# Strassen's seven products in 24 of 32 expanding feed-forward weight panels

## The chip, the cores and the metric

The kernel runs on one core of a Trainium2 chip. The metric is the device time of one execution in microseconds, the median of the runs. The kernel before took 2153.86 us (three runs, 2152.88 to 2155.65).

## The reference, cut to what matters

The program computes two transformer-like blocks on a stream of 512 tokens with 1024 features, all in float32. The first block has two layers (a convolution layer and a layer with forgetting attention), and each of them ends in a squared-ReLU feed forward:

```python
hn = rmsnorm(h, ffn_norm[i])
h = h + jnp.square(jax.nn.relu(hn @ ffn_w1[i])) @ ffn_w2[i]   # w1: 1024 x 4096, w2: 4096 x 1024
gate = jax.nn.sigmoid(rmsnorm(h, ple_norm[i]) @ ple_w_gate[i])
h = h + gate * (p[i] @ ple_w_proj[i])
```

The change lies in the product `hn @ ffn_w1[i]` of both layers. The second block (recurrence, block attention, memory attention, gated feed forward) is left as it was.

## The kernel before

The stream lies feature-major: eight tiles `h[f]` of 128 features x 512 tokens. Float32 products are made of three float32r products. Each operand is split into a high part, rounded to float32r, and a low part, the rest; `mm3` (line 356) issues weight-high x input-high, weight-high x input-low and weight-low x input-high into one accumulation in PSUM.

Weights come in panels of 128 x 2048 float32 (1 MB), in the order of the list `_KEYS`. A panel of `w1` holds 256 output features for all eight input tiles, so it takes 8 x 2 x 3 = 48 matmuls of 512 columns. `load` (299) issues a panel's DMA on the SP queue into one of two raw buffers. `part` (307) splits it a quarter at a time: ScalarE (ACT) copies the quarter into the high part, VectorE (DVE) subtracts to get the low part. High and low parts have two buffers each, so a panel is split while the one before it is multiplied, and `panel` (347) starts that for the next panel.

`ffn` (826) goes through four chunks of 1024 hidden features (c = 0 to 3) in each of the two layers. A chunk is four `w1` panels and then four `w2` panels. After each `w1` output tile DVE takes it out of PSUM (maximum with 0, times the norm's per-token factor `rbc`), ACT squares it, and ACT and DVE split the result for `w2`. Of `w2`, DVE adds each tile to the stream. `pairs` (379) runs the first panel of a group input tile by input tile for both output tiles at once (`couter`, 371), the others output tile by output tile.

The order of every engine's instructions is fixed when the program is built. `Flow` (124) keeps an estimated clock for each engine; side work (splitting, squaring, norms) is written as generators that name what their next step waits for, and each matmul issued lets those steps in that are due by the estimate. `quiet` (221) holds a step until an engine is about to be free, for at most `HOLD` us. On the chip each engine runs its list in order and waits by semaphores. Tiles of 128 x 512 come from one pool of `NSLOT` slots that are used in turn.

The products `p[i] @ ple_w_proj[i]` of both layers are made early, by `ple_proj` (700). Layer 0's eight tiles stay on chip, layer 1's go to DRAM (`prd`) and are read back after layer 1's feed forward.

Of the kernel before, what the change touches and what calls it, by code (L numbers as in the profile page):

```python
# [8 lines left out]
F32 = mybir.dt.float32  # L9
# [63 lines left out]
class Engine:  # L73
    """an engine whose instructions are issued in the order of the trace, with an estimate of when each one ends"""
# [152 lines left out]
def kernel(ctx: ExitStack, tc, gain0, x_t, p_t, mem_t, vec, w, w_f, w_lru, rows, consts, out):  # L227
# [69 lines left out]
    raws, parts = {}, {}  # L297

    def load(i, pieces=1):
        if i < len(_KEYS) and i not in raws:  # L300
            r = wp.tile([128, PW], F32, name=nm("raw"), tag="raw", bufs=2)
            raws[i] = r
            c = PW // pieces
            return [lambda k=k: dma(r[:, c * k:c * k + c], w[i, :, c * k:c * k + c]) for k in range(pieces)]
        return []

    def part(i, k, pieces, low):
        """piece k of a panel's split, its low part on engine low"""
        if k == 0:
            parts[i] = tuple(wp.tile([128, PW], F32R, name=nm(n), tag=n, bufs=2) for n in ("hi", "lo"))  # L310
        r, (hi, lo), c = raws[i], parts[i], PW // pieces
        s = slice(c * k, c * k + c)
        gain = GAINED.get(_KEYS[i][0])
        if gain is not None:
            g = col(gain, k)
            act.activation(hi[:, s], r[:, s], AF.Copy, scale=g)
            dve.scalar_tensor_tensor(lo[:, s], r[:, s], g, hi[:, s].bitcast(F32), op0=ALU.mult, op1=ALU.subtract)
        else:
            act.copy(hi[:, s], r[:, s])
            low.tensor_sub(lo[:, s], r[:, s], hi[:, s].bitcast(F32))  # L320

    def splitting(i):
        pieces = KT if _KEYS[i][0] in GAINED else 4
# [17 lines left out]
    def prefetch(i, delay):  # L341
        for g in load(i) + load(i + 1):
            g()
        if i < len(_KEYS) and _KEYS[i] not in FULL32:
            ahead[i] = flow.spawn(splitting(i), delay, 2)
# [1420 lines left out]
```

## Time and profile before

| | |
|---|---|
| median of three runs | 2153.86 us |
| profiled execution | span 2154.4 us, the only time shown for it |
| TensorE (PE) busy | 2109.2 us, 98% of the span, 9920 matmuls |
| VectorE (DVE) busy | 1270.6 us, 59% |
| ScalarE (ACT) busy | 937.4 us, 44% |
| GpSimd (POOL) busy | 370.5 us, 17% |
| granted TensorE clock, mean | 0.993 of full |
| DMA | 204.79 MB, queue q1 busy 26.8% |

A matmul's listed duration is its way through the array, and matmuls overlap: what a row of them costs is read from the distance between their starts, not from the sum of the durations. The same holds, by less, on DVE and ACT, where a merged row of four like instructions is shorter than four times one.

### The profile page before, as it was taken

The numbers are of one execution on the slowest core, as the hardware profiler recorded it, in microseconds if no ns is written. First come the engines' busy times: TensorE is split into PE (matmuls) and PEld (weight loads), VectorE is DVE, ScalarE is ACT, GpSimd is POOL, SyncE is SP. The second block draws the span as 40 slices with busy tenths as digits, with TensorE's granted clock in tenths as the row PEclk, the third lists the DMA queues.
The fourth block names the chain that finished last, engine by engine and source line by source line (L and its number), as shares of the span: only waits on it lengthen the run. The fifth ranks groups of instructions, "written<-read, shape, count | busy, mean of one in ns | idle before, by whom it ended". The sixth has DMA issues, their size and how long they took to land. (4 is left out here: it accounts for less than half of the span.)

```text
span 2154.4 us, 26102 instructions
## 1 busy us (share of the span) xinstructions
PE 2109.2 (98%) x9920; PEld 1741.6 (81%) x9920; DVE 1270.6 (59%) x2166; ACT 937.4 (44%) x1884; POOL 370.5 (17%) x380
## 2 busy tenths in 40 slices
PE   7999999999999999999999999999999999999998
PEld 6867888888878887788888887778888888888887
DVE  5997534344576887544343567775564556465563
ACT  5766423233446676433232453665452333232222
POOL 5881100000121336300000031331010010000002
PEclk9999999999999999999999999999999999999999
DMA  5215232232222111222222233112222422222221
GB/s 183 98 45 190 86 110 80 97 104 92 98 80 85 61 61 60 79 98 98 98 93 89 95 125 129 71 64 95 98 79 79 142 93 98 100 96 98 95 101 59
DMA packets 38444, 204.79 MB, mean 95 GB/s; under 512 B 4648, under 2 KB 7976, under 8 KB 15920
## 3 DMA queue, kind: packets, MB, share of 16 engines
q1 hardware_dynamic: 37744, 202.62, 26.8%
q8 instruction: 78, 1.28, 0.2%
q10 hardware_dynamic: 576, 0.52, 0.1%
q14 instruction: 46, 0.38, 0.1%
HBM read 195.45 MB, written 7.68 MB: 94 GB/s over the span
## 5 line engine op out<-in xcount | busy, mean ns | idle before, releaser
L83 PE MATMUL mm<-xh,hi 128*128 128x512 f32 (+1 forms) x2544 | 991.5, 390 | 9.3 <-ACT hi L83 8.4
L83 PE MATMUL mm<-xl,hi 128*128 128x512 f32 (+1 forms) x2544 | 990.5, 389 | 0.0
L83 PE MATMUL mm<-xh,lo 128*128 128x512 f32 (+1 forms) x2544 | 990.0, 389 | 0.2
L83 PEld LDWEIGHTS mm<-xh,hi 128*128 128x128 f32 x2544 | 480.2, 189 | 105.0 <-ACT hi L83 8.4
L83 PEld LDWEIGHTS mm<-xh,lo 128*128 128x128 f32 x2544 | 480.1, 189 | 96.5 <-DVE lo L83 1.5
L83 PEld LDWEIGHTS mm<-xl,hi 128*128 128x128 f32 x2544 | 480.2, 189 | 94.3
L83 ACT CAST hi<-raw 128x512 fp32r<-128x512 f32 x636 | 354.3, 616 | 288.6 <-PE mm L83 268.9
L83 DVE TENSOR_TENSOR lo<-raw,hi 128x512 fp32r<-128x512 f32 x584 | 387.9, 713 | 50.3 <-ACT hi L83 48.8
L83 POOL TENSOR_TENSOR sq<-sq,sq 128x512 f32<-128x512 f32 (+1 forms) x69 | 84.7, 1230 | 1330.0 <-ACT sq L83 1329.4
L83 DVE TENSOR_TENSOR h<-mm,h 128x512 f32<-128x512 f32 (+1 forms) x113 | 75.6, 671 | 279.7 <-PE mm L83 279.6
L83 ACT ACTIVATE z<-z 128x512 f32<-128x512 f32 x64 | 40.4, 631 | 205.3 <-DVE z L83 205.3
L83 DVE SCALAR_TENSOR_TENSOR z<-mm,rbc 128x512 f32<-128x512 f32 x64 | 44.0, 690 | 120.7 <-PE mm L83 120.7
L83 POOL TENSOR_SCALAR P<-P,s 128x128 f32<-128x128 f32 (+2 forms) x112 | 65.3, 588 | 243.6 <-DVE s L83 151.0
L83 DVE TENSOR_TENSOR t<-mm,rbc 128x512 f32<-128x512 f32 x80 | 54.9, 688 | 82.5 <-PE mm L83 78.7
L83 DVE TENSOR_TENSOR xl<-z,xh 128x512 fp32r<-128x512 f32 x64 | 44.3, 693 | 74.7 <-ACT xh L83 74.7
L83 ACT ACTIVATE t<-t 128x512 f32<-128x512 f32 x40 | 25.2, 631 | 128.5 <-DVE t L83 128.4
L83 POOL TENSOR_TENSOR acc<-acc,tap 128x482 f32<-128x482 f32 (+29 forms) x60 | 77.3, 1288 | 13.1 <-ACT tap L83 9.5
L83 DVE SCALAR_TENSOR_TENSOR sc<-u,V,sc 128x511 f32<-128x511 f32 (+21 forms) x116 | 78.9, 732 | 0.5
L83 ACT ACTIVATE xh<-h,V 128x512 fp32r<-128x512 f32 x40 | 28.6, 722 | 112.4 <-DVE h L83 112.4
L83 POOL TENSOR_TENSOR lo<-raw,hi 128x512 fp32r<-128x512 f32 x52 | 69.6, 1363 | 38.8 <-ACT hi L83 38.6
L83 ACT CAST pth<-ptp 128x128 fp32r<-128x128 f32 (+2 forms) x112 | 46.1, 418 | 53.2 <-PE ptp L83 52.6
L83 ACT ACTIVATE P<-sc,s 128x128 f32<-128x128 f32 (+2 forms) x112 | 58.5, 524 | 18.1 <-DVE s L83 17.4
(228 smaller groups left out, 2235.8 us busy)
## 6 DMA issues: line engine op xcount, KB each, us to landing
raw<-in_w SPq DMA_DIRECT2D x175, 1024.0 KB
h<-in_x_t SPq DMA_DIRECT2D x8, 256.0 KB
prd<-pr SPq DMA_DIRECT2D x8, 256.0 KB
pr<-prd SPq DMA_DIRECT2D x8, 256.0 KB
resid<-h SPq DMA_DIRECT2D x8, 256.0 KB
h<-resid SPq DMA_DIRECT2D x8, 256.0 KB
out<-out SPq DMA_DIRECT2D x12, 128.0 KB
raw<-in_w SPq DMA_DIRECT2D x4, 256.0 KB
```

The costliest lines, as they stand in the source:

```text
L83: f(out, *args, **kw)
```

## The change

Strassen's scheme multiplies 2 x 2 blocks with seven block products instead of eight, and pays with sums of blocks. Here the blocks are: of the inputs, the even and odd feature tiles times the two halves of 256 tokens; of a weight panel, its two output tiles times the even and odd input tiles. It is used for the `w1` panels of chunks 1 to 3 in both layers (`SEVEN`, 24 of 32). Chunk 0 keeps the old products, since the input sums are made meanwhile.

A panel's columns are now stored as four blocks of 512 columns (`blocks`, on the host, a permutation only). For a panel of `SEVEN`:

- `sums_split` makes four sums of blocks on DVE and splits them: four high parts on ACT, four low parts on DVE. Three blocks (a11, a12, a22) are also used alone; ACT makes their high parts.
- `lows_by_dma` makes those three blocks' low parts without DVE: ACT writes minus the rounded block into the low tile, and a DMA issued from POOL adds the block, read again from DRAM, to that tile (`accum_op=ALU.add`).
- `seven` issues seven products of four input tiles each, 3 matmuls of 256 columns per tile: 84 matmuls into three PSUM banks, of which two are added up in place. Between products ACT copies three half tiles out of PSUM, and DVE subtracts in PSUM twice, subtracts once on the way out, and applies the factor `rbc` to four half tiles.
- `combos` makes, once per layer during chunk 0, the sums of the inputs: for each of four pairs of tiles two scaled copies (ACT), four half-width sums (DVE), and the splits of two tiles.

High and low parts get one tile for each block (still two buffers). `NSLOT` grows from 60 to 64. Layer 0's `ple_proj` tiles go to DRAM as well, and both layers' are read back before the last chunk's `w2` panels (`pr_load`). Comments are dropped.

```diff
+    raws, parts, early = {}, {}, {}
 
     def load(i, pieces=1):
         if i < len(_KEYS) and i not in raws:
+            if _KEYS[i] in SEVEN:
+                early[i] = flow.spawn(lows_by_dma(i), 0.0, 2)
...
+    spent = set()
+    cur = [0]
+    def accumulate(out, src):
+        nc.gpsimd.dma_start(out, src, accum_op=ALU.add)
+        flow.dma_t = max(flow.dma_t, flow.now, flow.when([out])) + 4 * out.size() / 175e3
+        for k in flow.spans(out):
+            flow.ready[k] = flow.dma_t + 2.5
+    def lows_by_dma(i):
+        r = raws[i]
+        for b in range(3):
+            c = slice(S * b, S * b + S)
+            yield lambda: cur[0] >= i - 1 or (i - 2, b) in spent
+            yield r[:, c]
+            yield flow.quiet(act, patience=HOLD)
+            if i not in parts:
+                parts[i] = Panel(_KEYS[i])
+            lo = parts[i].piece("lo", b)
+            act.mul(lo, r[:, c], -1.0)
+            yield lo
+            accumulate(lo, w[i, :, c])
+    def sums_split(i):
+        if i not in parts:
+            parts[i] = Panel(_KEYS[i])
+        pan, r = parts[i], raws[i]
+        a11, a12, a22, a21 = (r[:, S * b:S * b + S] for b in range(4))
+        yield r
+        f1, f2, f3, f4 = (slot(p="sum") for _ in range(4))
+        pan.sums = tuple(mid(3 * S, F32R, n) for n in ("sh", "sl"))
+        def both(b):
+            return [t[:, S * b:S * b + S] for t in pan.sums]
+        s1, s2, s3, s4 = [pan.piece("hi", 3), pan.piece("lo", 3)], both(0), both(1), both(2)
+        pan.s1, pan.s2, pan.s3, pan.s4 = s1, s2, s3, s4
+        wait = lambda e: flow.quiet(e, patience=HOLD_SUMS)
+        yield wait(dve)
+        dve.tensor_add(f1, a21, a22)
+        yield wait(act)
+        act.copy(pan.piece("hi", 0), a11)
+        yield wait(dve)
+        dve.tensor_add(f2, f1, a11)
+        for f, (hi, lo), nxt, raw in (
+                (f2, s2, lambda: dve.tensor_add(f3, a11, a21), None),
+                (f1, s1, lambda: dve.tensor_add(f4, f2, a12), 1),
+                (f3, s3, None, 2), (f4, s4, None, None)):
+            yield f
+            yield wait(act)
+            act.copy(hi, f)
+            if nxt:
+                yield wait(dve)
+                nxt()
+            yield hi
+            yield wait(dve)
+            dve.tensor_sub(lo, f, hi.bitcast(F32))
+            if raw:
+                yield wait(act)
+                act.copy(pan.piece("hi", raw), r[:, S * raw:S * raw + S])
...
+    def combos(xs, src, g, out):
+        for j in range(KT // 2):
+            a, b = 2 * j, 2 * j + 1
+            yield lambda: xs[a] is not None and xs[b] is not None
+            yield [src[a], src[b], *xs[a], *xs[b]]
+            ga, gb = slot(p="ga"), slot(p="gb")
+            for t, f in ((ga, a), (gb, b)):
+                yield flow.quiet(act, patience=HOLD)
+                act.activation(t, src[f], AF.Copy, scale=g(f))
+            yield [ga, gb]
+            u, t = slot(p="u13"), slot(p="tu")
+            lh, rh = slice(0, HALF), slice(HALF, S)
+            for o, p, q, op in ((u[:, lh], ga[:, lh], ga[:, rh], dve.tensor_sub),
+                                (u[:, rh], ga[:, rh], gb[:, rh], dve.tensor_sub),
+                                (t[:, lh], gb[:, rh], u[:, lh], dve.tensor_add),
+                                (t[:, rh], gb[:, lh], t[:, lh], dve.tensor_sub)):
+                yield flow.quiet(dve, patience=HOLD)
+                op(o, p, q)
+            two = []
+            for z in (u, t):
+                zh, zl = slot(F32R, "ch"), slot(F32R, "cl")
+                yield z
+                yield flow.quiet(act, patience=HOLD)
+                act.copy(zh, z)
+                yield zh
+                yield flow.quiet(dve, patience=HOLD)
+                dve.tensor_sub(zl, z, zh.bitcast(F32))
+                two.append((zh, zl))
...
+    def seven(key, xs, cx, post):
+        pan = panel(key)
+        i = _PIDX[key]
+        lh, rh = slice(0, HALF), slice(HALF, S)
+        n = len(cx)
+        x = lambda f, h: [tuple(t[:, h] for t in xs[2 * j + f]) for j in range(n)]
+        y = lambda f, h: [tuple(t[:, h] for t in cx[j][f]) for j in range(n)]
+        block = lambda b: (pan.piece("hi", b), pan.piece("lo", b))
+        def product(ps, wt, bs, start):
+            for j in range(n):
+                c = slice(128 * j, 128 * j + 128)
+                a, b = (t[:, c] for t in wt)
+                p, q = bs[j]
+                pe.matmul(ps, a, p, start=start and j == 0, stop=False, skip_group_check=True)
+                pe.matmul(ps, a, q, start=False, stop=False, skip_group_check=True)
+                pe.matmul(ps, b, p, start=False, stop=j == n - 1, skip_group_check=True)
+        r1, r6 = bank()[:, :HALF], bank()[:, :HALF]
+        c1, c5 = slot(p="p1"), slot(p="n5")
+        c1, cw, c5 = c1[:, lh], c1[:, rh], c5[:, lh]
+        product(r1, block(0), x(0, lh), True)
+        spent.add((i, 0))
+        act.copy(c1, r1)
+        product(r6, pan.s2, y(1, lh), True)
+        full = bank("sc", 2)
+        r5 = full[:, :HALF]
+        dve.tensor_sub(r6, r6, c1)
+        act.copy(cw, r6)
+        product(r5, pan.s1, y(0, lh), True)
+        act.copy(c5, r5)
+        dve.tensor_sub(r5, r5, cw)
+        product(r1, block(1), x(1, lh), False)
+        spent.add((i, 1))
+        post(0, lh, r1)
+        product(r6, pan.s3, y(0, rh), False)
+        post(1, rh, r6, c5)
+        product(r5, pan.s4, x(1, rh), False)
+        post(0, rh, r5)
+        release("sc", full)
+        product(r6, block(2), y(1, rh), False)
+        post(1, lh, r6)
...
+            ahead[i] = flow.spawn(splitting(i), 0.2 if _KEYS[i] in SEVEN else delay, 2)
 
     def panel(key, fetch=True):
         i = _PIDX[key]
+        cur[0] = max(cur[0], i)
         if i not in ahead:
             ahead[i] = flow.spawn(splitting(i), 0.0, 2)
         flow.finish(ahead[i])
+        if i in early:
+            flow.finish(early[i])
...
+        cx = [None] * (KT // 2)
+        pr = None
         for c in range(4):
             z = [None] * KT
-            for k, ps in pairs([("w1", l, c, i) for i in range(4)], front.xs):
+            keys = [("w1", l, c, i) for i in range(4)]
+            for k, ps in pairs([q for q in keys if q not in SEVEN], front.xs):
                 rbc = front.get()
                 t = slot(p="z")
                 dve.scalar_tensor_tensor(t, ps, 0.0, rbc, op0=ALU.max, op1=ALU.mult)
                 flow.spawn(squared(z, k, t), 0.0, 0)
+                if c == 0 and k == 1:
+                    made = flow.spawn(combos(front.xs, h, front.g, cx), 0.0, 2)
+            if c == 0:
+                flow.finish(made)
+            for i, key in enumerate(keys):
+                if key not in SEVEN:
+                    continue
+                two = [slot(p="z") for _ in range(2)]
+                done = []
+                def post(j, half, ps, sub=None):
+                    t = two[j][:, half]
+                    if sub is not None:
+                        dve.tensor_sub(t, ps, sub)
+                        ps = t
+                    dve.scalar_tensor_tensor(t, ps, 0.0, front.rbc[:, half], op0=ALU.max, op1=ALU.mult)
+                    done.append(j)
+                    if done.count(j) == 2:
+                        flow.spawn(squared(z, 2 * i + j, two[j]), 0.0, 0)
+                seven(key, front.xs, cx, post)
+            if c == 3:
+                pr = pr_load(l)
...
+    def pr_load(l):
+        pr = []
+        for f in range(KT):
+            t = slot(p="pr")
+            dma(t, prd[KT * l + f])
+            pr.append(t)
+        return pr
...
-NSLOT = 60
+NSLOT = 64
...
+HOLD_SUMS = 0.6
+BLOCKED = ("w1",)
+SEVEN = {("w1", l, c, i) for l in range(2) for c in range(1, 4) for i in range(4)}
...
+    def blocks(m):
+        m = m.reshape(128, 4, 2, 2, 128)
+        return np.concatenate([m[:, :, o, t].reshape(128, 512) for o, t in ((0, 0), (1, 0), (1, 1), (0, 1))], axis=1)
...
-            return wide(a["ffn_w1"][key[1]], 1024 * key[2] + 256 * key[3], 256)
+            return blocks(wide(a["ffn_w1"][key[1]], 1024 * key[2] + 256 * key[3], 256))
```

In the orders below, `xh`, `xl` are the parts of the input tiles, `ch`, `cl` those of the input sums, `hi`, `lo` the parts of weight blocks, `sum` a weight sum before it is split, and `sh`, `sl` the parts of three of the four weight sums.

TensorE, the second `w1` panel of layer 0's chunk 1 in the kernel before, its first two input tiles:

```order
L83 MATMUL mm433_2662<-xh319_1775,hi428_2613 128x512
L83 MATMUL mm433_2662<-xl320_1776,hi428_2613 128x512
L83 MATMUL mm433_2662<-xh319_1775,lo429_2614 128x512
L83 MATMUL mm433_2662<-xh321_1777,hi428_2613 128x512
L83 MATMUL mm433_2662<-xl322_1778,hi428_2613 128x512
L83 MATMUL mm433_2662<-xh321_1777,lo429_2614 128x512
```

and the first panel of that chunk now: the end of the first product and the start of the second.

```order
L83 MATMUL mm598_2829<-xh417_1988,lo580_2740 128x256
L83 MATMUL mm598_2829<-xh434_2072,hi591_2760 128x256
L83 MATMUL mm598_2829<-xl435_2073,hi591_2760 128x256
L83 MATMUL mm598_2829<-xh434_2072,lo580_2740 128x256
L83 MATMUL mm599_2830<-ch470_2241,sh587_2753 128x256
L83 MATMUL mm599_2830<-cl471_2242,sh587_2753 128x256
L83 MATMUL mm599_2830<-ch470_2241,sl588_2754 128x256
L83 MATMUL mm599_2830<-ch493_2325,sh587_2753 128x256
L83 MATMUL mm599_2830<-cl494_2326,sh587_2753 128x256
L83 MATMUL mm599_2830<-ch493_2325,sl588_2754 128x256
```

Matmuls of 512 columns have become ones of 256, three for each pair of blocks as before; the second product takes sums on both sides, and its three parts take turns as those of the first do.

VectorE, from one output tile of the first `w1` panel of that chunk to the split of the second next panel, before:

```order
L83 SCALAR_TENSOR_TENSOR z430_2656<-mm426_2596,rbc365_2066 128x512
L83 SCALAR_TENSOR_TENSOR z431_2658<-mm427_2597,rbc365_2066 128x512
L83 TENSOR_TENSOR xl435_2667<-z430_2656,xh434_2666 128x512
L83 TENSOR_TENSOR xl437_2674<-z431_2658,xh436_2673 128x512
L83 TENSOR_TENSOR lo439_2689<-raw425_2594,hi438_2688 128x512 x4
L83 SCALAR_TENSOR_TENSOR z440_2707<-mm433_2662,rbc365_2066 128x512
L83 TENSOR_TENSOR xl443_2719<-z440_2707,xh442_2718 128x512
L83 SCALAR_TENSOR_TENSOR z444_2739<-mm441_2709,rbc365_2066 128x512
L83 TENSOR_TENSOR xl448_2751<-z444_2739,xh447_2750 128x512
L83 TENSOR_TENSOR lo450_2765<-raw432_2660,hi449_2764 128x512 x4
```

and now, the second panel's products and the third panel's sums and splits:

```order
L83 TENSOR_TENSOR mm625_2977<-mm625_2977,p1626_2978 128x256
L83 TENSOR_TENSOR xl638_3002<-z596_2826,xh637_3001 128x512
L83 TENSOR_TENSOR sl634_2990<-sum630_2986,sh633_2989 128x512
L83 TENSOR_TENSOR sc640_3028<-sc640_3028,p1626_2978 128x256
L83 TENSOR_TENSOR sum632_2988<-sum630_2986,raw597_2827 128x512
L83 TENSOR_TENSOR lo636_2992<-sum629_2985,hi635_2991 128x512
L83 SCALAR_TENSOR_TENSOR z621_2972<-mm624_2976,rbc453_2162 128x256
L83 TENSOR_TENSOR sl634_2990<-sum631_2987,sh633_2989 128x512
L83 TENSOR_TENSOR z622_2973<-mm625_2977,n5627_2979 128x256
L83 SCALAR_TENSOR_TENSOR z622_2973<-z622_2973,rbc453_2162 128x256
L83 TENSOR_TENSOR sl634_2990<-sum632_2988,sh633_2989 128x512
L83 SCALAR_TENSOR_TENSOR z621_2972<-sc640_3028,rbc453_2162 128x256
```

Between two panels stood two 512-wide outputs (`z`), two low parts of outputs (`xl`) and the four quarters of one panel. Now the half-wide steps on `mm` and `sc` stand between the sums and the low parts of the next panel, and each waits for its product while those behind it wait in the queue.

ScalarE in the same place, before:

```order
L83 ACTIVATE z430_2656<-z430_2656 128x512
L83 CAST xh434_2666<-z430_2656 128x512
L83 ACTIVATE z431_2658<-z431_2658 128x512
L83 CAST xh436_2673<-z431_2658 128x512
L83 CAST hi438_2688<-raw425_2594 128x512 x4
L83 ACTIVATE z440_2707<-z440_2707 128x512
L83 CAST xh442_2718<-z440_2707 128x512
L83 ACTIVATE z444_2739<-z444_2739 128x512
L83 CAST xh447_2750<-z444_2739 128x512
L83 CAST hi449_2764<-raw432_2660 128x512 x4
```

and now, in the first panel of the chunk:

```order
L83 COPY p1600_2831<-mm598_2829 128x256
L83 CAST sh609_2848<-sum606_2845 128x512
L83 COPY p1600_2831<-mm599_2830 128x256
L83 CAST hi611_2850<-sum605_2844 128x512
L83 COPY n5601_2832<-sc614_2881 128x256
L83 CAST hi615_2907<-raw578_2736 128x512
L83 CAST sh609_2848<-sum607_2846 128x512
L83 ACTIVATE lo616_2916<-raw597_2827 128x512
L83 CAST hi617_2925<-raw578_2736 128x512
L83 ACTIVATE lo618_2933<-raw597_2827 128x512
L83 CAST sh609_2848<-sum608_2847 128x512
L83 ACTIVATE z595_2825<-z595_2825 128x512
```

The three copies `p`, `p`, `n` from PSUM have come in, and the negative copies `lo<-raw` of the third panel (`raw597`) stand in the queue while the first panel is multiplied. The added DMAs follow each other on POOL, whose list in this place held nothing for the feed forward:

```order
L83 TENSOR_TENSOR s445_2135<-s444_2134,mhalf_78 128x4
L361 DMA lo580_2740<-in_w 128x512
L361 DMA lo581_2743<-in_w 128x512
L361 DMA lo582_2746<-in_w 128x512
L361 DMA lo602_2834<-in_w 128x512
L361 DMA lo603_2837<-in_w 128x512
L361 DMA lo604_2840<-in_w 128x512
```

The first row is the norm's factor; behind it stand three transfers for each panel.

## Rows read from the trace of the kernel before

**Rows 1.** the page: span, busy time by engine, granted TensorE clock in 40 slices

```profile
span 2154.4 us, 26102 instructions
PE 2109.2 (98%) x9920; PEld 1741.6 (81%) x9920; DVE 1270.6 (59%) x2166; ACT 937.4 (44%) x1884; POOL 370.5 (17%) x380
...
PEclk9999999999999999999999999999999999999999
```

**Rows 2.** waits, 250 to 600 us: waiter <- releaser, us, times, longest

```profile
DVE h L83 <- PE mm L83: 92.5, 25, 5.1
DVE z L83 <- PE mm L83: 58.9, 24, 7.1
...
PEld tp L83 <- POOL s L83: 0.4, 1, 0.4
```

**Rows 3.** timeline of TensorE, layer 0's feed forward: start, duration; 21 rows

```profile
379.32 0.39 PE L83 MATMUL mm<-xl,hi 128*128 128x512 f32 x1
...
383.85 0.39 PE L83 MATMUL mm<-xh,hi 128*128 128x512 f32 x1
```

**Rows 4.** timeline of TensorE in a stretch of 256-column matmuls; 59 rows

```profile
664.92 0.28 PE L83 MATMUL mm<-lo,xh 128*128 128x256 f32 x1
...
671.88 0.28 PE L83 MATMUL mm<-hi,xl 128*128 128x256 f32 x1
```

**Rows 5.** timeline of VectorE in two w1 panels: start, busy, idle before

```profile
359.57 0.69 DVE L83 SCALAR_TENSOR_TENSOR z<-mm,rbc 128x512 f32<-128x512 f32 x1 [2.71 <-PE mm L83]
...
370.45 0.69 DVE L83 SCALAR_TENSOR_TENSOR z<-mm,rbc 128x512 f32<-128x512 f32 x1 [2.71 <-PE mm L83]
372.49 0.69 DVE L83 TENSOR_TENSOR xl<-z,xh 128x512 fp32r<-128x512 f32 x1 [1.35 <-ACT xh L83]
373.10 2.49 DVE L83 TENSOR_TENSOR lo<-raw,hi 128x512 fp32r<-128x512 f32 x4
```

**Rows 6.** groups of VectorE: busy us, mean ns of one, idle before

```profile
L83 DVE TENSOR_TENSOR lo<-raw,hi 128x512 fp32r<-128x512 f32 x584 | 387.9, 713 | 50.3 <-ACT hi L83 48.8 <-DMA h<-resid 1.2
...
L83 DVE TENSOR_TENSOR xl<-z,xh 128x512 fp32r<-128x512 f32 x64 | 44.3, 693 | 74.7 <-ACT xh L83 74.7
...
L83 DVE TENSOR_TENSOR h<-xh,xl 128x512 f32<-128x512 f32 x4 | 6.2, 1607 | 0.0
...
L83 DVE SCALAR_TENSOR_TENSOR out<-h,V,tp 128x256 f32<-128x256 f32 x12 | 4.9, 476 | 3.2 <-ACT rbc L83 3.2
...
L83 DVE TENSOR_TENSOR h<-mm,h 128x256 f32<-128x256 f32 x8 | 3.4, 422 | 12.4 <-PE mm L83 12.4
```

**Rows 7.** timeline of ScalarE in the same panel as the last of rows 5

```profile
372.37 2.18 ACT L83 CAST hi<-raw 128x512 fp32r<-128x512 f32 x4
```

**Rows 8.** groups of ScalarE, columns as in rows 6

```profile
L83 ACT CAST hi<-raw 128x512 fp32r<-128x512 f32 x636 | 354.3, 616 | 288.6 <-PE mm L83 268.9 <-issue 18.6 <-DMA raw<-in_w 0.9
...
L83 ACT ACTIVATE z<-z 128x512 f32<-128x512 f32 x64 | 40.4, 631 | 205.3 <-DVE z L83 205.3
L83 ACT CAST xh<-z 128x512 fp32r<-128x512 f32 x64 | 39.8, 621 | 2.3
...
L83 ACT ACTIVATE xh<-h,V 128x512 fp32r<-128x512 f32 x40 | 28.6, 722 | 112.4 <-DVE h L83 112.4
...
L83 ACT CAST pth<-ptp 128x256 fp32r<-128x256 f32 x40 | 14.7, 372 | 25.0 <-PE ptp L83 24.9
```

**Rows 9.** busy time by stretch: PE, PEld, DVE, ACT, POOL, clock, DMA share, GB/s

```profile
250.00:600.00 350.00, 350.00 (x1553) 289.81 (x1552) 152.07 (x234) 119.31 (x210) 9.21 (x7) 1.00 0.28 96
353.00:364.00 11.00, 11.00 (x50) 9.10 (x49) 5.30 (x9) 4.59 (x8) 0.00 (x0) 1.00 0.26 97
...
344.00:348.00 4.00, 4.00 (x19) 3.34 (x18) 0.76 (x2) 1.25 (x2) 0.00 (x0) 1.00 0.74 262
```

**Rows 10.** the page's DMA issues: queue, count, KB each

```profile
raw<-in_w SPq DMA_DIRECT2D x175, 1024.0 KB
```

**Rows 11.** groups of GpSimd, columns as in rows 6

```profile
L83 POOL TENSOR_TENSOR s<-s,mhalf 128x4 f32<-128x4 f32 x10 | 12.8, 1284 | 53.6 <-DVE s L83 53.6
```

More of the change, by code (lines that the diff above doesn't have):

```diff
@@ L305, in load, with __init__, piece, cols @@
         return []
-    def part(i, k, pieces, low):
[L309 to L312, printed above, removed]
+    class Panel:
+        def __init__(self, key):
+            self.key, self.blocked = key, key[0] in BLOCKED
+            self.q = {}
+        def piece(self, n, b):
+            if (n, b) not in self.q:
+                self.q[n, b] = wp.tile([128, S], F32R, name=nm(n), tag=f"{n}{b}", bufs=2)
+            return self.q[n, b]
+        def cols(self, a, m):
+            return tuple(self.piece(n, a // S)[:, a % S:a % S + m] for n in ("hi", "lo"))
+        def weights(self, k, c0, width, m):
+            if self.blocked:
+                return self.cols(S * (c0 // 128 * (3 - k % 2) + (1 - c0 // 128) * (k % 2)) + k // 2 * 128, m)
+            return self.cols(k * width + c0, m)
+    class Plain:
+        def __init__(self, hi, lo):
+            self.hi, self.lo = hi, lo
+        def weights(self, k, c0, width, m):
+            a = k * width + c0
+            return self.hi[:, a:a + m], self.lo[:, a:a + m]
+    def part(i, k, pieces, low):
+        if i not in parts:
+            parts[i] = Panel(_KEYS[i])
+        c = PW // pieces
+        r = raws[i][:, c * k:c * k + c]
+        hi, lo = parts[i].cols(c * k, c)
         gain = GAINED.get(_KEYS[i][0])
@@ new lines, in sums_split @@
+    def sums_split(i):
+        if i not in parts:
+            parts[i] = Panel(_KEYS[i])
+        pan, r = parts[i], raws[i]
[30 more added lines that the diff above has]
+                act.copy(pan.piece("hi", raw), r[:, S * raw:S * raw + S])
@@ new lines, in combos @@
+    def combos(xs, src, g, out):
[26 more added lines that the diff above has]
+                two.append((zh, zl))
+            out[j] = two
@@ L322, in splitting @@
     def splitting(i):
+        if _KEYS[i] in SEVEN:
+            yield from sums_split(i)
+            return
         pieces = KT if _KEYS[i][0] in GAINED else 4
@@ L367, in gemm @@
                 flow.until(lambda: xs[k] is not None)
-            a = k * width + c0
-            mm3(ps, hi[:, a:a + m], lo[:, a:a + m], xs[k][0], xs[k][1], k == 0, k == n - 1)
+            wh, wl = pan.weights(k, c0, width, m)
+            mm3(ps, wh, wl, xs[k][0], xs[k][1], k == 0, k == n - 1)
     def couter(pan, xs, ks=None, banks=None):
@@ L688 @@
             conv_pe(k)
-    prd = dp.tile([KT, 128, S], F32, name="prd")
+    prd = dp.tile([2 * KT, 128, S], F32, name="prd")
     def gemm32(ps, raw, c0, xs, width, m=128):
@@ L715, in ple_proj @@
             act.copy(t, ps)
-            res.append(t)
-            if not keep:
-                dma(prd[f], t)
-            elif f in PLE_PE:
+            dma(prd[KT * l + f], t)
+            if l == 0 and f in PLE_PE:
                 conv_pe(PLE_PE[f])
-        return res
     memd = dp.tile([4, 128, S], F32, name="memd")
@@ L1271 @@
     front = Front(lambda f: gg[:, f:f + 1])
-    pr = []
-    for f in range(KT):
-        t = slot(p="pr")
-        dma(t, prd[f])
-        pr.append(t)
     def to_second(f):
```

34 lines of the change are left out of this document (16 added, 18 removed).

## The prediction

> **What bounds the kernel now.** First the page's head: TensorE is busy for 98% of the span, VectorE for 59%, ScalarE for 44%, and the clock slices stand at 9 throughout [rows 1]. Matmuls overlap, so a busy TensorE need not be a full one; the busy table of the first feed forward says more: from 250 to 600 us PE has work in all of the 350 us at a granted clock of 1.00 (the 2.4 GHz level), while DVE works 152 and ACT 119 us [rows 9]. Then the waits of that stretch: DVE waits for PE's sums (92.5 and 58.9 us in its two largest rows), and the only wait of the PE side is 0.4 us, in a norm [rows 2]. So in the feed forward nothing but the pace of the matmuls sets the time, and what the change takes off that pace comes off the span, as long as DVE, ACT and the transfers keep up.
>
> The pace itself is read from the timeline by starts. 512-column matmuls start every (383.85 - 379.32) / 20 = 0.2265 us [rows 3], and the same tile of two successive `w1` panels leaves at 359.57 and 370.45: 10.88 us per panel, 0.2267 for each of its 48 matmuls [rows 5]. 256-column matmuls of the same kind start every (671.88 - 664.92) / 58 = 0.120 us [rows 4], though every one of them has other weights than the one before it (high, low, high of the next tile). That is more than half of 0.2267: about 0.0133 us of each matmul does not shrink with its columns.
>
> **What the change removes on TensorE.** A panel of `SEVEN` had 48 matmuls of 512 columns, 10.88 us. It now has 7 products x 4 tiles x 3 = 84 of 256 columns: 84 x 0.120 = 10.08 us. The saving is 0.80 us, not the eighth (1.36 us) that the columns alone would give. 24 panels: 19.2 us. Nothing else on PE changes in number.
>
> **What it adds on VectorE, for each panel.** Before: 4 low parts, 2 outputs, 2 splits, 5.30 us of work in an 11 us window [rows 9]. Now 4 sums, 4 low parts of sums, 2 splits of outputs (10 full-width operations), 3 half-width subtractions and 4 half-width outputs. Price from below: four low parts in a row take 2.49 us, the last of them as long as a single one, 0.69, so each holds the engine (2.49 - 0.69) / 3 = 0.60 us [rows 5]; the half-width rows last 0.422 (two operands) and 0.476 us (three) [rows 6], less the same tail of 0.09 us 0.33 and 0.39. That is 10 x 0.60 + 3 x 0.33 + 4 x 0.39 = 8.6 us. From above, whole durations without overlap: 8 x 0.713 + 2 x 0.693 + 3 x 0.422 + 4 x 0.476 = 10.3 us. The panel's new pace on PE is 10.08, so DVE has either 1.5 us to spare or none. I take 8.6 (within a panel DVE's queue is mostly full, and back to back is then the right price), plus something for waits: the half-width steps wait for their products with sums queued behind them, as DVE's order shows.
>
> **On ScalarE, for each panel.** 3 negative copies, 3 plain high parts, 4 high parts of sums, 2 squares, 2 high parts of outputs (14 full-width), and 3 half-width copies from PSUM. From below: (2.18 - 0.62) / 3 = 0.52 us each [rows 7], and 0.372 - 0.095 = 0.28 for the half ones [rows 8]: 8.1 us. From above: 10 x 0.616 + 2 x 0.631 + 2 x 0.621 + 3 x 0.372 = 9.8 us. It fits below 10.08 in both cases; before it was 4.59 in 11 us [rows 9].
>
> **Hand-overs between products.** The tightest is bank r6: after the fifth product DVE must take r6 minus c5 out before the seventh adds to it. One product lies between, 12 x 0.120 = 1.44 us; the subtraction takes 0.42, so about 1.0 us is left for what stands ahead of it on DVE. One full-width operation (0.69) fits, a second costs PE some 0.4 us. For 24 panels this is between 0 and 10 us. I take 1.2 us (0.05 each): the order puts one low part and one half-width output between the neighbouring hand-overs, not two low parts. The other hand-overs have two products (2.9 us) or more.
>
> **The added transfers.** 3 per panel, 256 KB each, read and added to what is in SBUF, issued from POOL. The trace has no transfer that adds and none from POOL. From below: a plain 1 MB panel [rows 10] takes 0.74 x 4 us = 2.96 us of all 16 engines [rows 9], so 256 KB take 0.74 us. From above: four passes instead of one, 2.96 us, and in series with it an issue as long as the longest small POOL row, 1.28 us [rows 11], together 4.2 us. The middle that I take is two passes, 1.5 us.
>
> The Trainium skill, "Collectives: The Full Stack", section "The bandwidth ceiling: the fold count and why AG ≠ RS ≠ AR", says that an adding transfer is slower because it reads two sources, not because of the adding. By that page a transfer here would be an estimated 1.5 us; no row here shows it.
>
> At 1.5 us a panel needs 3 x 1.5 + 2.96 for the next raw panel = 7.5 of 10.08 us of the DMA engines; this fits. Latency doesn't matter: ACT's order shows the third panel's negative copies queued between the first panel's own copies, so a low part is started more than one panel (10 us) ahead of its product. On POOL nothing for the feed forward is queued behind these transfers; its busy time in the stretch is 9.21 us of 350 [rows 9].
>
> **Edits at nothing.** `combos`, once per layer: ACT 8 x 0.722 + 8 x 0.62 [rows 8] = 10.7 us, DVE 16 x 0.42 + 8 x 0.69 [rows 6] = 12.3 us, in a chunk 0 of 8 x 10.88 = 87 us where both engines are idle more than half of the time [rows 9]; should they wait, the first panel of chunk 1 is late by a part of that. Sixteen reloads and eight more stores of 256 KB, 6 us of transfers per layer, stand on SP ahead of a raw panel that is loaded a panel (10.88 us) early; DMA share there is 0.28 [rows 9]. At each chunk's end the last panel finishes both its output tiles together, but the first `w2` panel uses them last, 6 x 6 x 0.2267 = 8.2 us after it starts.
>
> **The sum.** 2154.4 (the profiled span; it stands 0.5 us above the median of the runs) - 19.2 + 1.2 = 2136.4, so about **2136 us**, 0.8% faster. Of this the pace of the matmuls is sure, the 1.2 us is judgement.
>
> **Rivals.**
>
> *VectorE sets the panel's pace.* For it: 8.6 us of work in 10.08 us, in strict order, behind hand-overs with ACT and PE at every second step; the low parts' mean of 0.713 us over 584 is above the 0.69 of one that runs alone [rows 6, 5]. Against it: between two groups of four such panels lie four `w2` panels, where DVE has slack. It decides from 10.08 us on. At the upper price with its waits, 10.6 us, a panel saves 0.28 instead of 0.80 us: 2154.4 - 6.7 = 2148.
>
> *The adding transfers set the pace: slower.* A chunk's 12 must pass in four panels and one panel of lead, 50.4 us, beside four raw panels of 2.96 us: (50.4 - 11.8) / 12 = 3.2 us each is where it decides. PE then waits for a low part at the head of a product. At the upper end of 4.2 us each of 6 chunks loses 12 x 1.0 = 12 us: 2136 + 72 = 2208. For it: both the adding and the issuing engine are unknown here, and a panel's whole margin is 7.2 us over three transfers. Against it: it needs more than four times the plain price.
>
> *DVE is held up by POOL's transfers: slower.* DVE's sum of two SBUF tiles lasted 1607 ns while POOL ran its own half of the same sums (`H_POOL`) [rows 6], 0.9 us above normal. If issuing a transfer does the same to one DVE operation, DVE needs 8.6 + 2.7 = 11.3 us a panel, 0.4 more than the old pace: 2154.4 + 24 x 0.42 = 2165.
>
> The Trainium skill, "SBUF — State Buffer", section "Who interferes with whom", has a DVE operation with two SBUF inputs collide with a POOL instruction that reads SBUF, not with one that only writes it, and says that `tensor_tensor` was not seen to hold up transfers from POOL. The 1.6 us row agrees with the first half; by the second this rival falls away. No run here shows it.
>
> *It does nothing:* the PE saving is met by waits of its size. No row speaks for just that.
>
> **Chances.** Forecast 0.68 (2132 to 2142), DVE's pace 0.14, slower by the adding transfers 0.10, slower by POOL's hold on DVE 0.04, nothing 0.04. A measurement of this kernel can tell about 0.2%, 4 us, from no change (the runs before spread over 2.8 us). Faster by that: the forecast and most of DVE's pace, 0.81. Within: the rest of it and the last case, 0.05. Slower: 0.14. The range goes from 2131 (no loss at all, less the 0.5 between span and median, and a spread of 3) to 2156, which takes in DVE's pace up to the upper price and leaves the two slower cases mostly out.
>
> **What would show it.** Right: 256-column matmuls 0.120 us apart in chunks 1 to 3; `mm` outputs of one panel to the next 10.1 us apart; no wait on the PE side for `lo`, `sl` or DVE's `mm`; DVE near 0.85 busy by starts. If PE waits for `lo` with POOL's transfers landing late, it is the second rival; if for `sh`, `sl` or `mm` with DVE full, the first; if DVE's own rows lengthen beside POOL's transfers, the third. The forecast is wrong if alternating 84 weight sets in three banks cannot keep 0.120 us.

## The result, and the profile after

| | median of the runs | span of the profiled run |
|---|---|---|
| before | 2154.76 us (2152.88 to 2157.23) | 2154.4 us |
| after | 2139.0 us (2138.45 to 2139.59) | 2136.4 us |

The changed kernel takes 0.9929 of the time before, 95% interval 0.9915 to 0.9943. The span fell by 18.0 us, the median by 15.8. The profiled span of before lies in the upper part of its spread: a run's time is its span and about 2 us more (2138.45 us for the 2136.4 of after), so a span of 2154.4 belongs to a run of some 2156.

The page of after, as in [rows 1], with the row of the queue that POOL issues to and its line among the DMA issues (count, KB each, median us from issue to landing):

```profile
span 2136.4 us, 28876 instructions
...
PE 2089.5 (98%) x10784; PEld 1766.9 (83%) x10784; DVE 1382.0 (65%) x2430; ACT 1062.4 (50%) x2132; POOL 432.0 (20%) x452
...
PEclk9999999999999999999999999999999999999999
...
q0 software_dynamic: 10368, 18.88, 5.5%
...
lo<-in_w POOLq DMA_DIRECT2D x72, 256.0 KB, 5.5
```

PE is as full as before with 864 more matmuls, DVE and ACT do 111 and 125 us more, and 72 adding transfers take 0.055 x 2136.4 / 72 = 1.63 us of all 16 engines each.

The timeline of TensorE at the first panel of seven products and at the next one; 83 rows lie between:

```profile
327.70 0.28 PE L83 MATMUL mm<-xh,hi 128*128 128x256 f32 x1
...
337.78 0.28 PE L83 MATMUL mm<-xh,hi 128*128 128x256 f32 x1
```

84 matmuls in 10.08 us are 0.120 us each, the distance that [rows 4] had in another stage; 48 took 10.88 us before [rows 5]. The busy table of that chunk, one panel of seven products per row and then the four `w2` panels (columns as in [rows 9]):

```profile
327.70:337.78 10.08, 10.08 (x86) 10.07 (x84) 8.05 (x15) 6.01 (x12) 2.35 (x3) 1.00 0.61 107
337.78:347.86 10.08, 10.08 (x87) 10.08 (x85) 8.85 (x17) 8.44 (x17) 2.61 (x3) 1.00 0.93 222
347.86:357.93 10.07, 10.07 (x86) 10.07 (x85) 8.80 (x17) 7.05 (x15) 0.86 (x1) 1.00 0.70 161
357.93:368.01 10.08, 10.08 (x86) 10.08 (x85) 6.49 (x13) 6.02 (x13) 0.00 (x0) 1.00 0.24 74
368.01:411.56 43.55, 43.55 (x194) 36.06 (x193) 18.76 (x30) 16.78 (x29) 4.54 (x6) 1.00 0.47 136
```

All four panels take the same time, though DVE's load, ACT's and that of the DMA engines differ from one to the next: none of the three sets the pace. The waits from 250 to 600 us have on the PE side the same single row as before, in the norm (0.5 us; before, 0.4 [rows 2]), and none in the panels. Who waits now is POOL, for ACT's negative copies, and DVE and ACT for PE's sums:

```profile
POOL lo L361 <- ACT lo L83: 240.7, 29, 69.4
DVE h L83 <- PE mm L83: 85.3, 25, 5.4
...
ACT hi L83 <- PE mm L83: 40.1, 21, 6.2
...
PEld tp L83 <- POOL s L83: 0.5, 1, 0.5
```

By the starts of the matmuls the 18 us lie where the prediction put them (us, each stretch to the next one's first matmul):

| stretch | before | after | difference |
|---|---|---|---|
| up to the first panel of seven products | 326.73 | 327.70 | +1.0 |
| six times four `w1` panels | 6 x 43.52 | 6 x 40.31 | -19.3 |
| six times four `w2` panels behind them | 6 x 43.52 | 6 x 43.55 | +0.2 |
| from there to layer 1's first such panel | 403.87 | 402.29 | -1.6 |
| from the last `w2` panel to the last matmul | 894.78 | 896.52 | +1.7 |

The rows outside the panels come to +1.3. Each is about as large as the difference between runs of one kernel: the spans of after's four runs go from 2136.4 to 2137.6.

### The profile page after: what moved, and what is told of

Read it like the earlier page. It is cut to its first block, busy times and chain, and to the rows that moved or that the text cites. A ratio compares the mean times of both kernels' runs of the same rounds, so it can differ in the third digit from the quotient of the medians.

```text
span 2136.4 us, 28876 instructions
## 1 busy us (share of the span) xinstructions
PE 2089.5 (98%) x10784; PEld 1766.9 (83%) x10784; DVE 1382.0 (65%) x2430; ACT 1062.4 (50%) x2132; POOL 432.0 (20%) x452
## 4 chain that ended last, share of the span: by engine, by line
PE 55%; DVE 4%; issue 1%; ACT 1%; DMA 0%; POOL 0%; DVEq 0%; SPq 0%; ACTq 0%; POOLq 0%
PE mm L83 51%; PE sc L83 3%; DVE lo L83 1%; DVE xc L83 1%; DVE xl L83 1%; PE ptp L83 1%; PE tp L83 1%; DVE s L83 0%; DVE h L83 0%; DMA mk<-memd 0%; POOL s L83 0%; DVE qq L83 0%; DVE sg L83 0%; DVE mg L83 0%; DVE ga L83 0%
## 5 line engine op out<-in xcount | busy, mean ns | idle before, releaser
L83 PE MATMUL mm<-xh,hi 128*128 128x512 f32 (+1 forms) x2352 | 897.8, 382 | 10.2 <-ACT hi L83 8.8
L83 PE MATMUL mm<-xh,lo 128*128 128x512 f32 (+1 forms) x2352 | 896.0, 381 | 6.8 <-DVE lo L83 6.6
L83 PE MATMUL mm<-xl,hi 128*128 128x512 f32 (+1 forms) x2352 | 895.6, 381 | 0.0
L83 PEld LDWEIGHTS mm<-xh,hi 128*128 128x128 f32 x2352 | 445.5, 189 | 91.2 <-ACT hi L83 8.8
L83 PEld LDWEIGHTS mm<-xh,lo 128*128 128x128 f32 x2352 | 445.4, 189 | 88.8 <-DVE lo L83 8.5
L83 PEld LDWEIGHTS mm<-xl,hi 128*128 128x128 f32 x2352 | 445.3, 189 | 79.7
L83 DVE TENSOR_TENSOR lo<-raw,hi 128x512 fp32r<-128x512 f32 x488 | 330.6, 719 | 58.2 <-ACT hi L83 56.7
L361 POOL DMA_DIRECT2D lo<-in_w x72 | 62.6, 895 | 481.2 <-ACT lo L83 479.2
L83 ACT ACTIVATE lo<-raw 128x512 fp32r<-128x512 f32 x72 | 44.9, 631 | 69.2 <-PE mm L83 69.2
```

What stands on the lines that cost most here:

```text
L83: f(out, *args, **kw)
L361: nc.gpsimd.dma_start(out, src, accum_op=ALU.add)
```

## The experiments

**All other edits without the seven products**

```diff
-SEVEN = {("w1", l, c, i) for l in range(2) for c in range(1, 4) for i in range(4)}
+SEVEN = set()
```

> All of the change but its products: SEVEN is empty, so every w1 panel runs as 48 matmuls of 512 columns, while the input sums of chunk 0, the column order of blocks, the tiles per block, the 64 slots and the stores and reloads of both layers' ple_proj tiles stay. Theory (the whole gain is the matmuls' pace, the other edits cost and give nothing): the kernel before, 2154.8, within 2 us; 192 matmuls of each w1 group again in 43.52 us. Rival (the slots, the reloads or the order of the other stages gave part of the gain): 2140 to 2150.

Measured: 2156.64 us against 2155.36 for before on the same chip, ratio 1.0006 (0.9997 to 1.0016), span 2154.9. The stored order of the columns, the larger `NSLOT`, the `ple_proj` tiles by way of DRAM and the reloads change nothing that can be measured. The whole gain is in the panels.

**Seven products in layer 0 only**

```diff
-SEVEN = {("w1", l, c, i) for l in range(2) for c in range(1, 4) for i in range(4)}
+SEVEN = {("w1", 0, c, i) for c in range(1, 4) for i in range(4)}
```

> The seven products in layer 0 alone, 12 panels. Theory: half of the pace's gain, 12 x 0.80 = 9.6 us below before, less what the other stages shift: 2145 to 2148, with 40.31 us for each group of four such panels and 43.52 for the groups of layer 1. Rival (a fixed loss or gain beside the products): further from the middle between 2154.8 and 2139.0 than 2 us.

Measured: 2148.59 us, ratio 0.9964 (0.9950 to 0.9977), span 2144.5: 9.9 us of span for 12 panels, 0.82 each, beside 18.0 for 24. The profiled run was the fastest of the five; by the medians it is 6.8 us beside 15.8, and 2148.59 lies 0.6 us above the range. In the panels themselves nothing differs from what was expected: by the starts four of them take 40.31 us in layer 0, and the 192 matmuls of a `w1` group of layer 1 again 43.52. The gain goes with the number of panels.

**The kernel before with halved matmuls.** In 18 `w1` panels of the kernel before, each product is issued as two of 256 columns; all else is as it was. This measures the disputed cost by itself: what half the columns cost without Strassen's sums and hand-overs.

```diff
-                    gemm(ps, pan, 128 * j, xs)
+                    halves = (slice(0, HALF), slice(HALF, S)) if key[0] == "w1" and key[2] > 0 else (slice(0, S),)
+                    for c in halves:
+                        gemm(ps[:, c], pan, 128 * j, [(p[:, c], q[:, c]) for p, q in xs])
```

> The kernel before, computing the same in the same steps but for one thing: in 18 w1 panels of chunks 1 to 3 each 512-column product is issued as two of 256 columns, first all of one token half and then all of the other, 96 matmuls a panel instead of 48. Theory (a matmul costs 0.120 us at 256 columns and 0.2267 at 512, so 0.0133 us of it do not shrink with its columns): 96 x 0.120 = 11.52 instead of 10.88 us a panel, 18 x 0.64 = +11.5 us over the kernel before, 2164 to 2169 us. Rival (time follows the columns, and 0.120 us holds only in the seven products because of what else runs there): no change to before, 2153 to 2158.

Measured: 2168.19 us against 2155.22, ratio 1.0064 (1.0049 to 1.0079), +13.0 by the medians and +10.0 by the profiled spans (2164.4). Its timeline of TensorE in such a panel, 17 rows:

```profile
350.06 0.28 PE L83 MATMUL mm<-xl,hi 128*128 128x256 f32 x1
...
351.98 0.28 PE L83 MATMUL mm<-xh,lo 128*128 128x256 f32 x1
```

1.92 / 16 = 0.120 us again. Halving the columns makes the same work dearer by 2 x 0.120 / 0.2267 = 1.059, so of the eighth that seven products save, less than 0.08 is left: 7/8 x 1.059 = 0.926, and 10.08 / 10.88 = 0.926.

**All low parts on DVE, no adding transfer**

```diff
-            if _KEYS[i] in SEVEN:
-                early[i] = flow.spawn(lows_by_dma(i), 0.0, 2)
...
+        yield pan.piece("hi", 0)
+        yield wait(dve)
+        dve.tensor_sub(pan.piece("lo", 0), a11, pan.piece("hi", 0).bitcast(F32))
...
+                yield pan.piece("hi", raw)
+                yield wait(dve)
+                dve.tensor_sub(pan.piece("lo", raw), r[:, S * raw:S * raw + S], pan.piece("hi", raw).bitcast(F32))
```

> The three low parts that ACT and an adding transfer make are made on VectorE by subtraction, as before; no transfer from GpSimd. VectorE then has 8.6 + 3 x 0.60 = 10.4 us of work in a panel of 10.08. Theory (VectorE had 1.5 us to spare and now lacks 0.3): up to 0.35 us a panel lost, less what the four w2 panels between give back: 2140 to 2148. Rival (VectorE was at its limit already, so the whole 1.8 us shows): 24 x 1.8 = 43 us, 2182. Second rival (its spare time is larger than the rows said): 2139, no wait of the PE side.

Measured: 2142.84 us, ratio 0.9937 (0.9921 to 0.9953), span 2141.1, 4.7 more than after. The waits of the PE side that after does not have (waiter <- releaser, us, times, longest):

```profile
PE mm L83 <- ACT p L83: 3.6, 6, 0.6
```

That is one wait per chunk, not one per panel. It lies in a chunk's fourth panel, which by the starts takes 10.95 us (356.86 to 367.81); the three ahead of it take 10.08 each. On TensorE:

```profile
363.39 0.39 PE L83 MATMUL mm<-ch,sh 128*128 128x256 f32 x1 [0.61 <-ACT p L83]
```

`p` is ACT's copy of bank r6 after DVE has subtracted in it, and DVE's timeline has that subtraction behind full-width rows that were queued up by then:

```profile
361.30 0.69 DVE L83 TENSOR_TENSOR lo<-raw,hi 128x512 fp32r<-128x512 f32 x1
361.90 0.68 DVE L83 TENSOR_TENSOR sl<-sum,sh 128x512 fp32r<-128x512 f32 x1
362.50 0.42 DVE L83 TENSOR_TENSOR mm<-mm,p 128x256 f32<-128x256 f32 x1
```

In after the same subtraction starts 3.2 us behind the head of its panel, here 5.6 us:

```profile
361.09 0.43 DVE L83 TENSOR_TENSOR mm<-mm,p 128x256 f32<-128x256 f32 x1 [1.37 <-PE mm L83]
```

So even with 1.8 us more of DVE work per panel (three low parts at 0.60) DVE does not set the pace of the first three panels; DVE falls behind, and one hand-over comes late in the fourth. By the trace this costs 6 x 0.87 = 5.2 us, so the adding transfers are worth about 0.2% here. The times alone would not show it: the interval of this ratio overlaps that of after (0.9915 to 0.9943).

**Two and three times the adding transfers**, the added ones into spare buffers that nobody reads. To make room both have 60 buffers of 256 KB instead of 64; a third kernel has those 60 alone.

```diff
+    spare = [cp.tile([128, S], F32, name=nm("spare")) for _ in range(4)]
...
+        for _ in range(1):        # 2 in the second kernel
+            spare.append(spare.pop(0))
+            nc.gpsimd.dma_start(spare[-1], src, accum_op=ALU.add)
...
-NSLOT = 64
+NSLOT = 60
```

> The changed kernel with 60 buffers of 256 KB instead of 64; nothing else is touched. It is the ground on which the two kernels with more adding transfers stand. Both theories: 2139 us (2136 to 2143), no PE wait in the panels of seven products, 10.08 us a panel.

> The changed kernel with each adding transfer issued twice, the second into spare buffers that nobody reads. By the time the transfers take in the trace after (0.055 x 2136.4 / 72 = 1.63 us of all 16 engines each) a chunk then has 24 x 1.63 + 4 x 2.96 = 51.0 us of transfers in the 50.4 us that four panels and one of lead give: just at its limit, so 2139 to 2150 us. If the price of a transfer were the 5.5 us from its issue to its landing, as if one had to end before the next begins, 24 would take 132 us a chunk and the span would grow by 6 x 80 = 480 us, to about 2620. If the transfers cost nothing that counts, 2139.

> The changed kernel with each adding transfer issued three times, two of them into spare buffers that nobody reads. At 1.63 us each a chunk has 36 x 1.63 + 4 x 2.96 = 70.5 us of transfers for 50.4 us: PE waits for low parts about 20 us a chunk, 120 us in all, 2259 us (2210 to 2300, less where the raw panels of the w2 stage are early enough). DMA share near 1.00 in the panels. If adding transfers have room beyond what their time in the trace says, 2139 to 2160.

Measured: 2139.32 us with 60 buffers alone, 2140.16 with twice the transfers (span 2138.8), 2192.51 with three times (ratio to before 1.0173, 1.0152 to 1.0193; span 2192.5). Twice as many are hidden. In its second and third panel PE is full while the DMA engines' share passes 1 (a share is summed over packets, and their times overlap), and a transfer now lands after 9.0 us instead of 5.5:

```profile
340.00:350.00 10.00, 10.00 (x86) 10.00 (x85) 8.65 (x17) 8.37 (x18) 5.08 (x7) 1.00 1.09 249
350.00:360.00 10.00, 10.00 (x86) 10.00 (x85) 7.61 (x15) 7.04 (x14) 0.36 (x1) 1.00 1.11 261
```

```profile
q0 software_dynamic: 20736, 37.76, 10.3%
...
lo<-in_w POOLq DMA_DIRECT2D x72, 256.0 KB, 9.0
```

Three times as many are not. The first row is from the waits of its PE side, the others are its busy table:

```profile
PE mm L83 <- DMA lo<-in_w: 35.6, 16, 4.7
```

```profile
340.00:350.00 10.00, 8.02 (x67) 7.81 (x66) 8.76 (x18) 8.36 (x17) 5.23 (x6) 1.00 1.10 272
350.00:360.00 10.00, 9.99 (x71) 10.00 (x72) 5.49 (x12) 4.76 (x10) 5.05 (x6) 0.83 1.11 217
360.00:370.00 10.00, 7.12 (x48) 6.91 (x47) 3.15 (x7) 3.06 (x7) 4.52 (x6) 0.83 1.10 259
```

PE waits for low parts, as the second rival described it, and loses more by the clock that falls behind the waits. The loss is 56 us, 9.4 a chunk, where 120 were expected (2210 at the least): a chunk's 36 transfers and four raw panels passed in 50.4 + 9.4 = 59.8 us, so a transfer costs at most (59.8 - 11.8) / 36 = 1.33 us when they crowd, less than the 1.63 of its packets' time. This is an upper bound, because POOL's list also waits for the four spare buffers; from 313 to 370 us:

```profile
POOL spare L367 <- DMA spare<-in_w: 20.7, 16, 3.7
```

How much of the loss is the DMA engines' (their share stands at 1.10 or 1.11 in the rows above) and how much these waits, and whether more spare buffers would hide 36 transfers, was not tried. The price from issue to landing, by which twice as many would have cost 480 us, counts for nothing.

**The tightest hand-over without its cover**

```diff
+        product(r6, block(2), y(1, rh), False)
+        post(1, lh, r6)
         product(r5, pan.s4, x(1, rh), False)
         post(0, rh, r5)
         release("sc", full)
-        product(r6, block(2), y(1, rh), False)
-        post(1, lh, r6)
```

> The changed kernel with the seventh product (bank r6) put ahead of the sixth, so that no product lies between the subtraction that takes r6 out (z<-mm,n, 0.42 us) and the next product into r6. Theory (a hand-over costs PE only what is not covered by the products between): PE now waits for that row in each panel, 0.42 us and the way to and from DVE, 0.6 us, up to 1.3 us where one full-width row stands ahead of it: 24 x 0.6 to 24 x 1.3 = 14 to 31 us, 2153 to 2170, with a PE wait for DVE z in the trace. Rival (the order of the hand-overs has no price, as the +1.2 us of the prediction would have it per 24 panels): 2139 to 2141.

Measured: 2158.14 us, ratio to before 1.0012 (1.0003 to 1.0022), span 2158.3: the order of two products is worth the whole gain. The wait and its place, on TensorE:

```profile
PE mm L83 <- DVE z L83: 13.7, 24, 0.7
```

```profile
334.02 0.28 PE L83 MATMUL mm<-ch,sl 128*128 128x256 f32 x1
334.82 0.39 PE L83 MATMUL mm<-ch,hi 128*128 128x256 f32 x1 [0.52 <-DVE z L83]
335.04 0.28 PE L83 MATMUL mm<-cl,hi 128*128 128x256 f32 x1
```

and on DVE:

```profile
334.34 0.42 DVE L83 TENSOR_TENSOR z<-mm,n 128x256 f32<-128x256 f32 x1 [0.41 <-PE mm L83]
```

From 334.02 to 335.04 two matmuls take 1.02 us instead of 0.24: 0.78 us a panel, of which the profile calls 0.52 a wait. 24 x 0.78 = 18.7 us; by the starts of all 24 panels it is 19.7, and the difference of the medians is 19.1. In after, the same DVE row has a whole product for its cover. The row on DVE and the head of the seventh product on TensorE:

```profile
335.10 0.42 DVE L83 TENSOR_TENSOR z<-mm,n 128x256 f32<-128x256 f32 x1 [0.42 <-PE mm L83]
```

```profile
336.34 0.28 PE L83 MATMUL mm<-ch,hi 128*128 128x256 f32 x1
```

It is done at 335.52, 0.8 us ahead of that product.

**More panels.** Chunk 0 keeps the old products because the input sums are made meanwhile. One kernel takes chunk 0's third and fourth panels too (28), another the fourth alone (26).

```diff
-SEVEN = {("w1", l, c, i) for l in range(2) for c in range(1, 4) for i in range(4)}
+SEVEN = {("w1", l, c, i) for l in range(2) for c in range(4) for i in range(4) if c > 0 or i > 1}   # 28
+SEVEN = {("w1", l, c, i) for l in range(2) for c in range(4) for i in range(4) if c > 0 or i > 2}   # 26
```

> Four panels more by seven products: the third and fourth of chunk 0 in both layers, so the input sums must be ready after the second panel. Theory (only the pace counts): 4 x 0.80 = 3.2 us below the change, 2136. Rival (the input sums, 12.3 us of VectorE and 10.7 of ScalarE beside the splits, are not done in the one panel left for them, and PE waits): each layer loses 3 us or more, 2139 to 2147.

> The changed kernel with the fourth panel of chunk 0 of each layer by seven products too, 26 panels. With 28 panels TensorE waited 10.7 us for the input sums (ch), which are made while the first panels of chunk 0 run. Theory (that loss is only a matter of when the sums are made; the fourth panel starts 10.88 us later than the third): no wait for ch, 2 x 0.80 = 1.6 us less than the 24 panels, 2135 to 2139. Rival (the sums are still late): a PE wait for ch of 1 to 5 us a layer, 2139 to 2150.

Measured: 2159.91 us with 28 panels (ratio to before 1.0018, 1.0007 to 1.0028; span 2157.9) and 2145.73 with 26 (0.9954, 0.9942 to 0.9967; span 2144.8). Both lose against 24, by 21 and 7 us. With 28, TensorE's timeline in layer 0, at the second product of the first such panel:

```profile
264.10 0.28 PE L83 MATMUL mm<-ch,sl 128*128 128x256 f32 x1
266.50 0.38 PE L83 MATMUL mm<-ch,sh 128*128 128x256 f32 x1 [2.12 <-ACT ch L83]
...
269.64 0.58 PE L83 MATMUL mm<-ch,sh 128*128 128x256 f32 x1 [1.46 <-ACT ch L83]
...
272.78 0.58 PE L83 MATMUL mm<-ch,sh 128*128 128x256 f32 x1 [1.62 <-ACT ch L83]
```

Each of the remaining three pairs of input tiles is late. The rival of the expectation described this, but 2159.91 lies far above its range: its price was 3 us a layer and more, while by the starts this panel takes 20.39 us instead of 10.08. The granted clock of the stretch with the waits is 0.63:

```profile
264.00:277.00 13.00, 7.01 (x27) 5.43 (x26) 10.59 (x22) 9.53 (x18) 1.74 (x2) 0.63 0.30 90
```

With 26 only the last pair is, and still:

```profile
277.55 0.39 PE L83 MATMUL mm<-ch,sh 128*128 128x256 f32 x1 [1.51 <-ACT ch L83]
278.27 0.58 PE L83 MATMUL mm<-cl,sh 128*128 128x256 f32 x1 [0.34 <-DVE cl L83]
...
281.43 0.32 PE L83 MATMUL mm<-xh,hi 128*128 128x256 f32 x1
```

```profile
274.50:277.50 3.00, 1.53 (x13) 1.33 (x12) 2.94 (x7) 2.29 (x5) 0.00 (x0) 1.00 0.88 270
277.50:281.40 3.90, 3.51 (x15) 3.32 (x16) 1.12 (x2) 0.64 (x2) 0.00 (x0) 0.57 0.15 61
281.40:285.00 3.60, 3.60 (x32) 3.60 (x31) 2.85 (x6) 2.45 (x5) 0.00 (x0) 0.99 0.00 0
```

A wait of 1.5 us is followed by 3.9 us at a granted clock of 0.57 (most of it at the lower level, 1.2 GHz), in which 15 matmuls take 3.88 us instead of 1.80, with a second wait of 0.34 us among them. So a wait of 1.5 us costs more than twice its length, and the 0.80 us that a panel saves does not pay for it. Of the 7 us between 26 and 24 panels the wait and this stretch make (1.7 + 2.1 - 0.8) x 2 = 6. The input sums would have to be made earlier; that was not tried. By the medians none of the kernels run is faster than the changed one.

## Why the prediction was right, point by point

- *PE's pace, -19.2 us.* Measured 40.31 us for four panels, 3.21 less than before, six times: -19.3. The distance of 0.120 us, read in another stage of the kernel before, held to the last digit in the panels and in the halved matmuls of the kernel before. The remark that every matmul has other weights than the one before it was misread: in the order of [rows 4], as in the panels, two matmuls in a row use the same block and the third another. What every matmul has is a weight load of its own (PE and PEld both x10784), and no run here tells what part of the 0.0133 us belongs to the load. It was the 0.120 us of [rows 4] that kept the forecast from taking the eighth, 1.36 us a panel, that the count of columns gives.
- *Hand-overs, +1.2 us.* The sum needed this term, but not for its reason. In the panels hand-overs cost nothing: 40.31 us are 336 x 0.120, and no PE wait lies in them. The +1.3 us that did appear lies outside the panels, in stretches that the prediction had at nothing, and is as large as the spread between runs. That the term came out is luck. What the prediction said of r6 was right in kind: the cover of one product leaves 0.8 us (forecast 1.0), and without it each panel loses 0.78 us.
- *VectorE, 8.6 us a panel, rival at 10.1 and more.* Busy 8.05, 8.85, 8.80 and 6.49 us in the four panels. The sum describes the second and the third: the first has no outputs of a panel before it to split, and the fourth prepares a `w2` panel. Their 8.8 is near the low end of the range. Back to back was the right price. The first rival falls, and with three more low parts a panel it still does not come about as a pace, only as one late hand-over per chunk.
- *ScalarE, 8.1 us.* Busy 8.44 and 7.05 us in the second and third panel, 6.9 in the mean of the four.
- *Adding transfers, 1.5 us between 0.74 and 4.2.* 1.63 us by the page of after, 10.3% x 2138.8 / 144 = 1.53 with twice as many, at most 1.33 when they crowd. The estimate of 1.5 us by two source reads from the Trainium skill ("Collectives: The Full Stack", section "The bandwidth ceiling: the fold count and why AG ≠ RS ≠ AR"), which speaks of reduce-scatter there, agrees with the first two. A chunk's 12 transfers are moved at no cost, 24 too, and 36 are not: PE then waits for low parts as the second rival has it, though part of that can come from the four spare buffers, and where the limit lies above 24 is open. The mean load was roughly as forecast (0.74 of the DMA engines; 0.62 over the four panels), the peak was not: 0.93 in the second panel, where transfers and the next raw panel meet. The margin given beside that rival is 10.08 - 2.96 = 7.1 us, not 7.2.
- *POOL's hold on DVE.* It falls. Of the 72 rows in which DVE makes low parts `sl` of weight sums, 18 overlap an issue on POOL and last 681 to 686 ns, no longer than the rest (shortest, median and longest duration of all 72 in ns), and here such a row of 0.68 us runs into an issue of 0.86 us on POOL:

```profile
L83 DVE TENSOR_TENSOR sl<-sum,sh x72: 678/683/694, 319.7 to 1178.2; 128x512 fp32r<-128x512 f32 x72
```

```profile
334.00 0.68 DVE L83 TENSOR_TENSOR sl<-sum,sh 128x512 fp32r<-128x512 f32 x1
```

```profile
334.51 0.86 POOL L361 DMA_DIRECT2D lo<-in_w  x1 [6.18 <-ACT lo L83]
```

  The Trainium skill, "SBUF — State Buffer", section "Who interferes with whom", has `tensor_tensor` not hold up transfers from POOL; this trace agrees, and shows that the issue does not hold up the operation either, here one with two SBUF inputs.
- *Edits at nothing.* Without seven products the kernel is as fast as before (1.0006). `combos` is hidden where it stands, with some 50 us to spare: its last row on DVE starts at 277.39 us, and the first product that takes an input sum starts at 329.14. In chunk 0's own last panel it would not be: the 26-panel kernel, which needs the last pair at 276 us, finds it 1.5 us late.

```profile
277.39 0.68 DVE L83 TENSOR_TENSOR cl<-tu,ch 128x512 fp32r<-128x512 f32 x1
```

```profile
329.14 0.28 PE L83 MATMUL mm<-ch,sh 128*128 128x256 f32 x1
```

- *The sum.* 2154.4 - 19.2 + 1.2 = 2136.4 is a span, and the span came out at 2136.4. As a time it lacked what lies around the span, 2.05 us in the run profiled after, and so the forecast of 2136 stands 3.0 us below the median of 2139.0. The step that failed is "it stands 0.5 us above the median of the runs": the only figure shown for the profiled run of before was its span, and the sentence took that for a time.

## What to carry to other kernels

Price a scheme that trades fewer columns for more and narrower matmuls by the distance between starts of matmuls of the new width, wherever in the trace they stand: here 7/8 of the columns were 0.926 of the time. Where TensorE is the bound, look for what covers each hand-over between an accumulating bank and another engine: here one product of 1.44 us was enough, and none cost 0.8 us each time, so that moving one product by one place cost as much as the scheme gained. Cover also depends on what is queued ahead on the other engine: with three more low parts a panel on VectorE, two products were too few once per chunk. Do not widen a scheme to panels whose inputs are just late: a wait of 1.5 us on TensorE cost more than twice that here, the rest mostly by the clock behind it.

## What the runs showed of the hardware

- Matmuls start every 0.2267 us at 512 columns and every 0.120 us at 256, with a weight load for each one: 0.0133 us of each pair do not shrink.
- A transfer of 256 KB that adds to SBUF, issued from POOL, takes 0.86 us of POOL, 1.5 to 1.6 us of all 16 DMA engines by its packets' time, at most 1.33 us when they crowd, and lands 5.5 us after its issue, 9.0 when twice as many are under way.
- After a wait of 1.5 us on TensorE in a full stretch the granted clock was 0.57 for the next 3.9 us; with a wait of 0.52 us in every panel of the reordered kernel, its busy table shows a granted clock of 1.00:

```profile
340.00:350.00 10.00, 9.48 (x79) 9.28 (x79) 7.95 (x17) 7.66 (x16) 1.76 (x3) 1.00 0.75 175
```
